# A hybrid mixer and expert layer: x is also given by channels, and the first norm's root is applied to the products' outputs

## The chip, the core and the metric

The kernel runs on one core of a Trainium2 chip. The metric is the device time of one execution in microseconds (us); what is compared are medians of several executions. The core's engines each work through a queue of their own in program order: TensorE (PE; its weight loads, PEld, overlap its products), VectorE (DVE), ScalarE (ACT), GpSimd (POOL) and SyncE (SP, which here only issues DMAs). They wait for each other by semaphores. Products land in PSUM, everything else lives in SBUF.

## What is computed

One layer over 1024 tokens of 1024 channels, in float32:

```python
hn = rmsnorm(x, norm_mix)                       # x * rsqrt(mean(x*x) + eps) * g
proj = hn @ w_in                                # 6160 columns: z, xbc, dt, sc_b, sc_c, sc_v
xbc = silu(causal_conv4(xbc) + b)               # 1536 channels: xs, B, C of the scan
dt  = softplus(dt_raw + dt_bias)                # 16 heads
y   = ssd_scan(xs, dt, -exp(a_log), B, C) + d_skip * xs
ssd = grouped_rmsnorm(y * silu(z), 2 groups)
sc  = grouped_rmsnorm(sc_b * causal_conv3(sc_c * sc_v), 16 groups)
h   = x + concat(ssd, sc) @ w_out
hn2 = rmsnorm(h, norm_ffn)                      # router: best of 4 groups, best 2 of its 8 experts
out = rmsnorm(h + sum_of_two(gate * expert(hn2)), final_norm)
```

The root of the first norm is one number per token. A product's output is linear in it, so it can be applied before the product, to x, or after it, to the outputs; `norm_mix` is one number per channel and goes onto x either way.

## The kernel before, in words

**Halves and blocks.** The tokens are worked in two halves of 512 (`TB`). A half of the mixer is 61 blocks, built by `add_blocks` (lines 123 to 143): one for `dt`, 12 for `xbc`, 24 for `c`, `v`, `b` (two each in turn), 8 for `z`, and 16 for `w_out` (`s` and `d`, four and four). A block is 24 products of 128x128 by 128x512 (the `dt` block has 16 narrow ones). Each matrix element is split into a high and a low half (`split_w`, lines 159 to 169: ACT copies the high half, DVE subtracts for the low half), and three products, high-high, high-low, low-high, make up one (`mm_block`, lines 255 to 260). The first half's blocks are 0 to 60, the second half's 61 to 121; blocks 62 to 73 are the second half's conv blocks, 75 the second of its `c` blocks.

**The order.** The loop at line 918 writes the order of every engine by hand. In step n it emits, in this order: `xbc_silu` of the conv output before last; the post step of block n-1 (`xbc_post` and so on, line 916); block n's products; the load of the weights to come and `split_w(n + 3)`; then the list `todo[n]`, filled by `at(n, function)` in lines 861 to 914, where `b0` is 1 for the first half and 62 for the second. PSUM has four banks for block outputs (`acc`), three for everything small (`sd`) and one (`sm`); weights have four buffers `W0` to `W3`, and `temp()` has four buffers too. So PE can run about three blocks ahead of the engines that empty its banks and split its weights, and not further.

**The conv blocks.** `xbc_post` (lines 365 to 379): ACT's `Identity` reads the block's output in PSUM with the last tap and the bias, then DVE adds the other three taps by three `scalar_tensor_tensor` (`stt`, line 84), in the second half also three short ones for the history. `dt_turn` and `dt_soft` (lines 306 to 342) make the step sizes, `cum_mm` and `cum_out` (346 to 362) their running sums. While the second half's conv blocks run, the first half's routing is done on the same engines (`h_root`, `h_rows`, `h_cols`, `route_choose`, `route_gates`, `route_pos`; `e0` is 64).

**The scan.** Per 128 tokens and group, `ssd_t` transposes, `ssd_decay` (ACT) makes the decay, `ssd_e` (DVE) the operands, `ssd_m` the products, `ssd_post` (DVE) the sums, one step each (lines 866 to 872). The first `ssd_m` of the second half stands behind block 77.

**The short conv.** `c_post` (391) copies a block to SBUF on ACT, `v_post` multiplies it in; `sc_root` (427 to 435) takes the root of the group sums, writes it to HBM and reads it back over all partitions (`rb_d` to `RB`); `sc_norm_out` waits for that.

**x.** It is read in three places. At the start four loads bring the first half by rows (`load_x`, 103); per 128 tokens ACT sums the squares, root and reciprocal follow, DVE scales the rows (`prep_stats`, `prep_root`, `prep_scale`, 226 to 234), and PE transposes them 128x128 at a time (`transpose_in`, 240, for `XT`), the eight groups of four interleaved with the `dt` products (288 to 299). For the second half the same is done at b0+46 to b0+59 of the first. And the residual: `x_load` (573) loads 128 columns of x by rows into ring 0, `x_turn` (576) transposes them on PE and copies them to ring 1 on ACT, and `o_post` (583) adds the block of `w_out` to them; `h_turn` (612) turns the sum back to rows.

**After the mixer** come 32 experts, whose weights (6 MB each) are loaded ahead by `load_m` and `reuse` (825 to 845) into every region that has come free, through the same SP queue that loads x and the weights before.

The root, as it stands in the kernel before:

```python
def inv_root(o, i, n):
    act.activation(o, i, AF.Sqrt, bias=eps[:o.shape[0]], scale=1.0 / n)
    dve.reciprocal(o, o)
def halves(o, k, pt, scale):
    copy_a(o[:, 0, k], pt, scale=scale)
    stt(o[:, 1, k], pt, scale, o[:, 0, k].bitcast(F32), OP.mult, OP.subtract)
```

Of the kernel before, what the change touches and what calls it, by code (L numbers as in the profile page):

```python
# [11 lines left out]
AF = mybir.ActivationFunctionType  # L12
OP = mybir.AluOpType
# [22 lines left out]
@with_exitstack  # L36
def layer(ctx: ExitStack, tc: tile.TileContext, x, norm_mix, w_in, ssd_conv_w, ssd_conv_b, dt_bias,
          a_log, d_skip, ssd_norm, sc_conv_w, sc_norm, w_out, norm_ffn, w_router_group,
          w_router_expert, w_gate, w_up, w_down, final_norm, out):
    nc = tc.nc  # L40
    x, out = x[0], out[0]
    w_in, w_out = w_in[0], w_out[0]
# [8 lines left out]
    def C(shape, name, dt=F32):  # L51
        return cst.tile(shape, dt, name=name)

    def region(tag, shape, dt=F32):
        return rg.tile(shape, dt, name=tag, tag=tag)

    def temp():
        return tk.tile([P, 512], F32, name="tk")

    def junk():  # L60
        return tk.tile([P, D], BF, name="junk", tag="tk")
# [4 lines left out]
    def sd_bank():  # L66
        return ps.tile([P, 512], F32, name="sd", bufs=3)
# [30 lines left out]
    acc_d = dr.tile([T, D], F32, name="acc_d")  # L98


    X = {}

    def load_x(h, tag):
        t = region(tag, [P, NT, D])
        for i in range(NT):
            sp.dma_start(t[:, i], x[h * TB + i * P:h * TB + (i + 1) * P, :])
        return t

    X[0] = load_x(0, "SC")
    prow = temp()  # L110
    prow = prow[:, :P]
    for o, n, src in ((0, 8, norm_mix), (8, 48, ssd_conv_w), (56, 12, ssd_conv_b), (68, 8, ssd_norm),
                      (76, 24, sc_conv_w), (100, 8, sc_norm), (108, 8, norm_ffn)):
        sp.dma_start(prow[o:o + n, :], bass.AP(tensor=src.tensor, offset=src.offset, ap=[[P, n], [1, P]]))

    WR = region("WR", [P, 2, 2048])
    W = [region(f"W{i}", [P, 2, 1024], FR) for i in range(4)]

# [26 lines left out]
    def load_w(s):  # L145
        if s < len(loads):
            src, k = loads[s]
            n = k * src.shape[1]
            sp.dma_start(WR[:, s % 2, 0:n].rearrange("p (k c) -> p k c", k=k), src.rearrange("(k p) c -> p k c", p=P))
# [19 lines left out]
            tt(o[1], raw_w(b), o[0].bitcast(F32), OP.subtract)  # L169

    load_w(0)
    load_w(1)
    dtb = C([P, H], "dtb")
    av = C([P, H], "av")
    dsk = C([P, H], "dsk")
# [41 lines left out]
    g2 = C([P, D], "g2")  # L217
    lg = C([P, NT, 36], "lg")

    pc = C([P, 116], "pc")  # L220

    def PC(i):
        return pc[:, i:i + 1]


    def prep_stats(h, i, o=None):
        act.activation(junk() if o is None else o, X[h][:, i], AF.Square, accum_out=ssx[:, h * 4 + i:h * 4 + i + 1])

    def prep_root(h, a, b):
        s = slice(h * 4 + a, h * 4 + b)  # L230
        inv_root(rsx[:, s], ssx[:, s], D)

    def prep_scale(h, i):
        dve.tensor_scalar(X[h][:, i], X[h][:, i], rsx[:, h * 4 + i:h * 4 + i + 1], None, op0=OP.mult)

    def halves(o, k, pt, scale):
        copy_a(o[:, 0, k], pt, scale=scale)
# [37 lines left out]
                pe.matmul(o[i], t[:, 1, k, c], w[:, 0, q], start=False, stop=k == KD - 1)  # L275


    pt = sd_bank()
    pe.transpose(pt[:, 0:116], prow[0:116, :], ident[0:116, 0:116])
    sq = region("Y", [P, NT, D])  # L280
    for i in range(NT):
        prep_stats(0, i, sq[:, i])
        prep_root(0, i, i + 1)
        prep_scale(0, i)
    dve.tensor_copy(pc, pt[:, 0:116])
    XT[0] = region(TA_IN[0], [P, 2, KD, TB], FR)
    DT0 = acc_bank()
    for k in range(KD):
        transpose_in(X[0], k, XT[0], PC(k))
        if k == 0:  # L290
            split_w(0)
            load_w(2)
        elif k == 4:
            split_w(1)
        if k > 1:
            mm_dt(DT0, 0, XT[0], k - 2)
    split_w(2)
    for k in (KD - 2, KD - 1):
# [20 lines left out]
    def dt_soft(h, pt):  # L319
        dts = temp()  # L320
        dt1, dt2, dt3 = (dts[:, i * 64:(i + 1) * 64] for i in range(3))
        pv = pt[:, :128].rearrange("p (c h) -> p c h", c=NT)
        tt(v64(dt1), pv[:, :, 0:H], b64(dtb), OP.add)
        tt(v64(dt1), v64(dt1), pv[:, :, H:2 * H], OP.add)
        stt(dt2, dt1, -1.0, dt1, OP.mult, OP.min)
        act.activation(dt2, dt2, AF.Exp)
        if h == 0:
            act.activation(av, av, AF.Exp)
            dve.tensor_scalar(av, av, -1.0, None, op0=OP.mult)
        dve.tensor_scalar(dt3, dt2, 1.0, None, op0=OP.add)  # L330
# [34 lines left out]
    def xbc_post(h, i, pt):  # L365
        o = XB[h][:, i]

        def w(q):
            return PC(8 + q * 12 + i)

        act.activation(o, pt, AF.Identity, bias=PC(56 + i), scale=w(3))
        for s in (1, 2, 3):
            stt(o[:, s:], pt[:, :TB - s], w(3 - s), o[:, s:], OP.mult, OP.add)
        if h == 0:
            dve.tensor_copy(hist[:, i], pt[:, TB - 3:])
        else:
# [13 lines left out]

    def c_post(h, j, pt):
        CSB[j] = temp()
        copy_a(CSB[j], pt)

    def v_post(h, j, pt):
        t = U["cv"][:, j % 2]
# [29 lines left out]

    def sc_root(h):
        gs = temp()[0:16, :]
        inv_root(gs, SUM.pop(h)[0:16, :], 64)
        pool.dma_start(rb_d[h * 16:(h + 1) * 16, :], gs)  # L430
        RB[h] = region("P1", [P, KD, TB])
        for s in range(2):
            src = rb_d[h * 16 + s:h * 16 + s + 1, :]
            pool.dma_start(RB[h][s * 64:(s + 1) * 64],
                           bass.AP(tensor=src.tensor, offset=src.offset, ap=[[0, 64], [2 * TB, KD], [1, TB]]))
# [90 lines left out]
    def z_post(h, j, pt):  # L526
        if j % 4 == 3:
            for i in range(NT):
                zs = temp()
                act.activation(zs, pt[i], AF.Silu)  # L530
                y = Y[h][:, i, j // 4 * 512:(j // 4 + 1) * 512]
                tt(y, y, zs, OP.mult)

# [37 lines left out]
        return t[h * TB:(h + 1) * TB, j * P:(j + 1) * P].rearrange("(i p) c -> p i c", p=P)  # L571

    def x_load(h, j):
        sp.dma_start(rows(ring(0, j)), dram_cols(x, h, j))

    def x_turn(h, j):
        pt = sd_bank()
        xr = ring(0, j)
        for i in range(NT):
            pe.transpose(pt[:, i * P:(i + 1) * P], xr[:, i * P:(i + 1) * P], ident)  # L580
        copy_a(ring(1, j), pt)

    def o_post(h, j, pt):
        tt(ring(1, j), ring(1, j), pt, OP.add)
# [276 lines left out]
    for h in range(2):  # L861
# [4 lines left out]
        for u in range(8):  # L866
# [15 lines left out]
        at(b0 + 43, o_room, h)  # L882
        for j in range(8):
            nd = b0 + 48 + j + (4 if j > 3 else 0)
            at(nd - 2, x_load, h, j)
            at(nd - 1, x_turn, h, j)
        if h == 1:
            for q, n in enumerate((44, 44, 45, 46, 51, 47, 49, 55, 56, 57, 57, 58, 58)):
                at(b0 + n, load_m, q)
            at(b0 + 50, h_diag)  # L890
        if h == 0:
            at(b0 + 46, lambda: X.__setitem__(1, load_x(1, "SC")))
            for i in range(NT):
                at(b0 + 50 + i // 2, prep_stats, 1, i)
            at(b0 + 52, prep_root, 1, 0, 4)
            for i in range(NT):
                at(b0 + 53, prep_scale, 1, i)
            at(b0 + 56, lambda: XT.__setitem__(1, region(TA_IN[1], [P, 2, KD, TB], FR)))
            for k in range(KD):
                at(b0 + 56 + k // 2, lambda k=k: transpose_in(X[1], k, XT[1], PC(k)))  # L900
            at(b0 + 28, route_load)
            at(b0 + 37, route_const)
            at(b0 + 46, route_weights)
            e0 = b0 + HB + 2
            at(e0 + 1, h_root, 0)
# [409 lines left out]
```

## Time and profile before

| | |
|---|---|
| median of 3 executions | 1434.77 us (1433.69 to 1438.48) |
| profiled execution | 1434.36 us, of which the span 1432.5 us |
| granted TensorE clock, mean over the span | 0.985 |
| PE, DVE, ACT, POOL busy | 95%, 72%, 63%, 10% |
| HBM read, written | 309.04 MB, 29.49 MB |

A row of the timeline is start, duration, engine, line of the kernel, operation, out<-in, shapes, count; what is in brackets is the idle time of the engine just before and what ended it. Rows of like instructions that follow each other are merged. A product's duration runs to its modelled end and overlaps the next one, so the cost of a product is the distance of two starts. `tt`, `stt` and `copy_a` are helpers, so that L87, L84 and L81 stand for many places: the tile names tell them apart. A tile is named by its region: P stands for the regions P1 and P2 (`seg`, `xw`, the rings), SC, Y, TA, TB for theirs, `tk` for a temp.

### The profile page before, as it was taken

How to read it: one execution, taken by the hardware profiler on the slowest of the kernel's cores; microseconds unless marked ns; L12 is line 12 of the kernel's file. 1: busy time of each engine (PE TensorE's matmuls, PEld its weight loads, DVE VectorE, ACT ScalarE, POOL GpSimd, SP SyncE). 2: the span in 40 equal slices, each digit the busy share in tenths (PEclk: the TensorE clock that was granted, in tenths of full speed). 3: DMA queues.
4: the chain of work that ended last, by engine and by line, in shares of the span. 5: the costliest groups of instructions: out<-in, count | busy, mean ns of one | idle time of the engine just before them, and what ended most of it. 6: DMA issues, size and time to landing. Idle time of an engine off the chain costs nothing. (4 is left out here: it accounts for less than half of the span.)

```text
span 1432.5 us, 17523 instructions
## 1 busy us (share of the span) xinstructions
PE 1364.8 (95%) x6467; PEld 1080.3 (75%) x6467; DVE 1036.5 (72%) x1357; ACT 895.4 (63%) x1344; POOL 139.0 (10%) x128
## 2 busy tenths in 40 slices
PE   6999999999999999999999699999999999999992
PEld 4888888878878878888788576777777777777771
DVE  5755676664367776755643588999999999999884
ACT  5655434355465644343643577788888888888884
POOL 0000010200000000000000101211111111111110
PEclk9999999999999999999999899999999999999996
DMA  6323332453444232324655779899999999997996
GB/s 193 134 91 115 102 108 89 117 179 106 138 153 134 89 118 89 103 89 126 227 188 168 277 294 339 317 361 361 356 372 364 351 360 378 387 375 275 367 369 249
DMA packets 130533, 322.67 MB, mean 225 GB/s; under 512 B 11039, under 2 KB 91091, under 8 KB 105868
## 3 DMA queue, kind: packets, MB, share of 16 engines
q1 hardware_dynamic: 117164, 291.06, 55.7%
q0 software_dynamic: 13280, 30.45, 8.4%
q8 instruction: 52, 0.85, 0.2%
q14 instruction: 37, 0.30, 0.1%
HBM read 309.04 MB, written 29.49 MB: 236 GB/s over the span
## 5 line engine op out<-in xcount | busy, mean ns | idle before, releaser
L87 DVE TENSOR_TENSOR W<-WR,W 128x1024 fp32r<-128x1024 f32 (+1 forms) x162 | 195.2, 1210 | 108.5 <-ACT W L81 108.2
L1150 PE MATMUL acc<-W,TB 128*112 128x512 f32 x512 | 205.3, 401 | 0.0
L1151 PE MATMUL acc<-W,TB 128*112 128x512 f32 x512 | 201.6, 394 | 2.7 <-DVE W L87 2.7
L1152 PE MATMUL acc<-W,TB 128*112 128x512 f32 x512 | 203.3, 397 | 0.0
L81 ACT ACTIVATE W<-WR 128x1024 fp32r<-128x1024 f32 (+1 forms) x162 | 168.4, 1043 | 34.1 <-PE acc L275 18.3
L258 PE MATMUL acc<-TA,W 128*128 128x512 f32 x416 | 165.5, 398 | 2.0 <-ACT tk L530 2.0
L258 PE MATMUL acc<-TB,W 128*128 128x512 f32 x416 | 166.0, 399 | 1.4 <-ACT tk L530 1.4
L260 PE MATMUL acc<-TA,W 128*128 128x512 f32 x416 | 162.3, 390 | 0.0
L260 PE MATMUL acc<-TB,W 128*128 128x512 f32 x416 | 162.3, 390 | 0.0
L259 PE MATMUL acc<-TA,W 128*128 128x512 f32 x416 | 162.1, 390 | 0.0
L259 PE MATMUL acc<-TB,W 128*128 128x512 f32 x416 | 162.0, 389 | 0.0
L87 DVE TENSOR_TENSOR W<-SC,W 128x1024 fp32r<-128x1024 f32 x96 | 114.3, 1219 | 16.7 <-ACT W L81 16.4
L87 DVE TENSOR_TENSOR W<-Y,W 128x1024 fp32r<-128x1024 f32 x92 | 109.4, 1218 | 11.5 <-ACT W L81 11.4
L1151 PEld LDWEIGHTS acc<-W,TB 128*112 128x112 f32 x512 | 90.3, 176 | 32.0 <-DVE W L87 3.6
L1152 PEld LDWEIGHTS acc<-W,TB 128*112 128x112 f32 x512 | 89.6, 175 | 29.5 <-DVE TB L87 0.2
L1150 PEld LDWEIGHTS acc<-W,TB 128*112 128x112 f32 x512 | 89.8, 175 | 27.5 <-ACT TB L81 0.2
L1162 PE MATMUL sd<-W,TB 128*112 128x512 f32 x256 | 101.3, 396 | 3.2 <-DVE W L87 3.2
L81 ACT ACTIVATE W<-SC 128x1024 fp32r<-128x1024 f32 x96 | 98.4, 1058 | 9.4 <-PE sd L1163 2.4
L87 DVE TENSOR_TENSOR W<-P,W 128x1024 fp32r<-128x1024 f32 x80 | 95.3, 1218 | 12.5 <-ACT W L81 12.5
L1161 PE MATMUL sd<-W,TB 128*112 128x512 f32 x256 | 103.5, 404 | 0.6 <-ACT TB L81 0.6
L1163 PE MATMUL sd<-W,TB 128*112 128x512 f32 x256 | 101.7, 397 | 0.0
L81 ACT ACTIVATE W<-Y 128x1024 fp32r<-128x1024 f32 x92 | 94.8, 1059 | 10.8 <-PE sd L1163 3.9
(316 smaller groups left out, 2486.3 us busy)
## 6 DMA issues: line engine op xcount, KB each, us to landing
WR<-in_w_in_dram SPq DMA_DIRECT2D x44, 1024.0 KB, 5.0
SC<-in_w_down_dram SPq DMA_DIRECT2D x18, 1024.0 KB, 7.4
WR<-in_w_out_dram SPq DMA_DIRECT2D x16, 1024.0 KB, 6.6
SC<-in_w_gate_dram SPq DMA_DIRECT2D x16, 1024.0 KB, 7.6
P<-in_w_up_dram SPq DMA_DIRECT2D x16, 1024.0 KB, 7.6
Y<-in_w_up_dram SPq DMA_DIRECT2D x16, 1024.0 KB, 8.0
Y<-in_w_gate_dram SPq DMA_DIRECT2D x15, 1024.0 KB, 8.3
TA<-in_w_down_dram SPq DMA_DIRECT2D x15, 1024.0 KB, 6.8
```

Source lines behind the costliest of these rows:

```text
L81: act.activation(o, i, AF.Copy, scale=scale)
L87: dve.tensor_tensor(o, a, b, op=op)
L258: pe.matmul(o, w[:, 0, k], t[:, 0, k], start=start and k == 0, stop=False)
L259: pe.matmul(o, w[:, 0, k], t[:, 1, k], start=False, stop=False)
L260: pe.matmul(o, w[:, 1, k], t[:, 0, k], start=False, stop=stop and k == KD - 1)
L1150: pe.matmul(pt, a[:, 0, k], w[:, 0, q], start=k == 0, stop=False)
L1151: pe.matmul(pt, a[:, 0, k], w[:, 1, q], start=False, stop=False)
L1152: pe.matmul(pt, a[:, 1, k], w[:, 0, q], start=False, stop=k == KD - 1)
L1161: pe.matmul(pt, a[:, 0, k], w[:, 0, n], start=k == 0, stop=False)
L1162: pe.matmul(pt, a[:, 0, k], w[:, 1, n], start=False, stop=False)
L1163: pe.matmul(pt, a[:, 1, k], w[:, 0, n], start=False, stop=k == 3)
```

## The change

x is passed to the kernel a second time as its transpose (`xT`, 1024 channels by 1024 tokens), and the small vectors as one 128x116 table (`small`). Both are laid out before the launch. The tokens' high and low halves (`XT`) are made straight from the loaded channels with `norm_mix`, without the norm's root. The rows of x are still loaded, for the sums of squares only: the first half's into region Y behind the first weights, the second half's into P2 at the start too. `root_rows` spreads the root over all partitions (a diagonal of it times a matrix of ones) and keeps it and its square in `ROOT`, which lies in the buffer of `g2`; `g2` is loaded later, once per half (`g2_load`, split off `route_load`). The root is then applied to the outputs of the blocks: `xbc`, `dt` and `z` by the root, `c` by its square (for `c` times `v`), and the group sums of the short conv by both (for `b`). The residual is loaded by channels into ring 1.

```diff
--- before.py
+++ after.py
+    pc = C([P, 116], "pc")
+    sp.dma_start(pc, small)
...
+    def load_xT(h, k, n):
+        sp.dma_start(X[h][:, k:k + n], xT[k * P:(k + n) * P, h * TB:(h + 1) * TB].rearrange("(k p) t -> p k t", p=P))
+
+    def load_rows(h, tag):
+        t = ROWS[h] = region(tag, [P, NT, D])
         for i in range(NT):
             sp.dma_start(t[:, i], x[h * TB + i * P:h * TB + (i + 1) * P, :])
...
+    X[0] = region("SC", [P, KD, TB])
...
     load_w(0)
+    for k in range(KD):
+        load_xT(0, k, 1)
     load_w(1)
+    load_rows(0, "Y")
...
-    def prep_scale(h, i):
-        dve.tensor_scalar(X[h][:, i], X[h][:, i], rsx[:, h * 4 + i:h * 4 + i + 1], None, op0=OP.mult)
+    ROOT = g2.rearrange("p (s t) -> p s t", s=2)
+
+    def root_rows(h):
+        pt = sd_bank()
+        for i in range(NT):
+            d = temp()[:, 0:P]
+            dve.tensor_scalar(d, ident, rsx[:, h * 4 + i:h * 4 + i + 1], None, op0=OP.mult)
+            pe.matmul(pt[:, i * P:(i + 1) * P], ones, d, start=True, stop=True)
+        copy_a(ROOT[:, 0], pt)
+        act.activation(ROOT[:, 1], pt, AF.Square)
...
-    for i in range(NT):
-        prep_stats(0, i, sq[:, i])
-        prep_root(0, i, i + 1)
-        prep_scale(0, i)
...
-        transpose_in(X[0], k, XT[0], PC(k))
+        halves(XT[0], k, X[0][:, k], PC(k))
...
+    for i in range(NT):
+        prep_stats(0, i)
+    prep_root(0, 0, 4)
+    root_rows(0)
+    load_rows(1, "P2")
...
-        tt(v64(dt1), pv[:, :, 0:H], b64(dtb), OP.add)
-        tt(v64(dt1), v64(dt1), pv[:, :, H:2 * H], OP.add)
+        r = rsx[:, h * 4:h * 4 + 4][:, :, None].to_broadcast([P, NT, H])
+        tt(v64(dt1), pv[:, :, 0:H], r, OP.mult)
+        tt(v64(dt2), pv[:, :, H:2 * H], r, OP.mult)
+        tt(v64(dt1), v64(dt1), b64(dtb), OP.add)
+        tt(dt1, dt1, dt2, OP.add)
...
+        t = temp()
+        tt(t, pt, ROOT[:, 0], OP.mult)
+        pt = t
         act.activation(o, pt, AF.Identity, bias=PC(56 + i), scale=w(3))
...
-        copy_a(CSB[j], pt)
+        tt(CSB[j], pt, ROOT[:, 1], OP.mult)
...
-        inv_root(gs, SUM.pop(h)[0:16, :], 64)
+        tt(gs, SUM.pop(h)[0:16, :], ROOT[0:16, 1], OP.mult)
+        inv_root(gs, gs, 64)
+        tt(gs, gs, ROOT[0:16, 0], OP.mult)
...
-                act.activation(zs, pt[i], AF.Silu)
+                act.activation(zs, pt[i], AF.Silu, scale=rsx[:, h * 4 + i:h * 4 + i + 1])
...
-        sp.dma_start(rows(ring(0, j)), dram_cols(x, h, j))
-    def x_turn(h, j):
-        pt = sd_bank()
-        xr = ring(0, j)
-        for i in range(NT):
-            pe.transpose(pt[:, i * P:(i + 1) * P], xr[:, i * P:(i + 1) * P], ident)
-        copy_a(ring(1, j), pt)
+        sp.dma_start(ring(1, j), xT[j * P:(j + 1) * P, h * TB:(h + 1) * TB])
...
+        at(b0 + 40, g2_load)
+        if h:
+            at(b0, root_rows, 1)
...
-            at(nd - 2, x_load, h, j)
-            at(nd - 1, x_turn, h, j)
+            at(nd - 1, x_load, h, j)
...
-            at(b0 + 46, lambda: X.__setitem__(1, load_x(1, "SC")))
+            at(b0 + 46, lambda: X.__setitem__(1, region("SC", [P, KD, TB])))
+            at(b0 + 46, load_xT, 1, 0, 4)
+            at(b0 + 46, load_xT, 1, 4, 4)
...
-                at(b0 + 50 + i // 2, prep_stats, 1, i)
-            at(b0 + 52, prep_root, 1, 0, 4)
-            for i in range(NT):
-                at(b0 + 53, prep_scale, 1, i)
+                at(b0 + 2 + i, prep_stats, 1, i)
+            at(b0 + 6, prep_root, 1, 0, 4)
...
-                at(b0 + 56 + k // 2, lambda k=k: transpose_in(X[1], k, XT[1], PC(k)))
+                at(b0 + 56 + k // 2, lambda k=k: halves(XT[1], k, X[1][:, k], PC(k)))
```

## Rows read from the trace of the kernel before

**Rows 1.** page, part 1: busy us (share of the span) xinstructions of each engine

```profile
PE 1364.8 (95%) x6467; PEld 1080.3 (75%) x6467; DVE 1036.5 (72%) x1357; ACT 895.4 (63%) x1344; POOL 139.0 (10%) x128
```

**Rows 2.** waits of PE, 0 to 790 us: who waited for whom: total, times, longest

```profile
PE acc L258 <- ACT tk L530: 3.4, 2, 2.0
...
PE sd L580 <- DVE TA L84: 0.7, 1, 0.7
...
PE sd L466 <- DVE Y L87: 0.5, 1, 0.5
```

**Rows 3.** windows: stretch, length, busy us (xinstructions), PEclk, DMA share, GB/s

```profile
60.00:98.00 38.00, 38.00 (x170) 31.45 (x169) 23.77 (x35) 16.59 (x22) 0.00 (x0) 1.00 0.37 124
450.00:495.00 45.00, 45.00 (x224) 37.55 (x223) 41.40 (x101) 21.09 (x29) 1.65 (x3) 1.00 0.33 110
```

**Rows 4.** timeline of PE at the first half's last `d` blocks

```profile
379.08 0.60 PE L580 MATMUL sd<-ident,P 128*128 128x128 f32 x4
379.44 0.48 PE L258 MATMUL acc<-TA,W 128*128 128x512 f32 x1
...
385.44 1.04 PE L243 MATMUL sd<-ident,SC 128*128 128x128 f32 x8
386.23 0.48 PE L258 MATMUL acc<-TA,W 128*128 128x512 f32 x1
```

**Rows 5.** timeline of PE: the first product of block 1

```profile
24.25 0.39 PE L258 MATMUL acc<-TA,W 128*128 128x512 f32 x1
```

**Rows 6.** windows of the start

```profile
2.00:6.00 4.00, 0.00 (x0) 0.00 (x0) 0.09 (x1) 1.80 (x6) 1.69 (x3) 1.00 0.93 350
6.00:11.50 5.50, 0.00 (x0) 0.00 (x0) 2.65 (x6) 2.65 (x6) 0.00 (x0) 1.00 0.81 138
11.50:13.00 1.50, 0.00 (x0) 0.00 (x0) 0.02 (x1) 1.44 (x3) 0.00 (x0) 1.00 0.14 30
```

**Rows 7.** timeline of ACT at the start: the last sum of squares

```profile
11.53 1.06 ACT L227 ACTIVATE Y<-SC 128x1024 f32<-128x1024 f32 x1 [0.99 <-DMA SC<-in_x_dram]
```

**Rows 8.** timeline of PE: block 75 begins; first `ssd_m` of the second half

```profile
487.34 0.49 PE L258 MATMUL acc<-TB,W 128*128 128x512 f32 x1
...
506.17 1.89 PE L497 MATMUL sd<-P,P 128*128 128x64 f32 x16
```

**Rows 9.** windows at the change from mixer to experts

```profile
806.40:816.90 10.50, 2.34 (x21) 2.04 (x20) 5.63 (x26) 5.13 (x17) 1.11 (x1) 0.50 0.68 251
816.90:820.00 3.10, 3.06 (x12) 2.44 (x13) 1.34 (x4) 1.09 (x2) 0.00 (x0) 0.50 0.02 5
```

**Rows 10.** timeline of DVE, second half, conv blocks to first `v` block

```profile
449.80 2.32 DVE L84 SCALAR_TENSOR_TENSOR TA<-acc,pc,TA 128x511 f32<-128x511 f32 x3 [2.39 <-ACT TA L371]
...
481.55 2.31 DVE L84 SCALAR_TENSOR_TENSOR TA<-acc,pc,TA 128x511 f32<-128x511 f32 x3
...
485.92 2.32 DVE L84 SCALAR_TENSOR_TENSOR TA<-acc,pc,TA 128x511 f32<-128x511 f32 x3 [0.29 <-ACT TA L371]
...
504.20 0.69 DVE L87 TENSOR_TENSOR P<-sd,dtt 128x512 f32<-128x512 f32 x1
...
506.06 0.68 DVE L87 TENSOR_TENSOR P<-acc,tk 128x512 f32<-128x512 f32 x1
...
507.54 0.75 DVE L84 SCALAR_TENSOR_TENSOR SC<-P,pc,SC 128x512 f32<-128x512 f32 x1 [0.79 <-ACT SC L81]
```

**Rows 11.** lines by form, 413.5 to 520 us: group xcount | busy, mean ns | idle

```profile
L84 DVE SCALAR_TENSOR_TENSOR TA<-acc,pc,TA 128x511 f32<-128x511 f32 x12 | 9.0, 747 | 8.6 <-ACT TA L371 8.6
...
L84 DVE SCALAR_TENSOR_TENSOR SC<-P,pc,SC 128x512 f32<-128x512 f32 x4 | 3.0, 752 | 2.5 <-ACT SC L81 2.4
...
L626 ACT ACTIVATE junk<-P 128x128 bf16<-128x128 f32 x6 | 1.8, 308 | 0.2
...
L81 ACT ACTIVATE tk<-acc 128x512 f32<-128x512 f32 x2 | 1.2, 578 | 0.0
```

**Rows 12.** waits of the whole run: DVE for the broadcast root

```profile
DVE SC L84 <- DMA P<-rb_d: 5.4, 2, 3.4
```

More of the change, by code (lines that the diff above doesn't have):

```diff
@@ L38, in layer @@
           a_log, d_skip, ssd_norm, sc_conv_w, sc_norm, w_out, norm_ffn, w_router_group,
-          w_router_expert, w_gate, w_up, w_down, final_norm, out):
+          w_router_expert, w_gate, w_up, w_down, final_norm, xT, small, out):
     nc = tc.nc
@@ L98, in layer, with PC @@
     acc_d = dr.tile([T, D], F32, name="acc_d")
+    pc = C([P, 116], "pc")
+    sp.dma_start(pc, small)
+    def PC(i):
+        return pc[:, i:i + 1]
     X = {}
-    def load_x(h, tag):
-        t = region(tag, [P, NT, D])
+    def load_xT(h, k, n):
+        sp.dma_start(X[h][:, k:k + n], xT[k * P:(k + n) * P, h * TB:(h + 1) * TB].rearrange("(k p) t -> p k t", p=P))
+    ROWS = {}
+    def load_rows(h, tag):
+        t = ROWS[h] = region(tag, [P, NT, D])
         for i in range(NT):
             sp.dma_start(t[:, i], x[h * TB + i * P:h * TB + (i + 1) * P, :])
[L107 to L114, printed above, removed]
+    X[0] = region("SC", [P, KD, TB])
     WR = region("WR", [P, 2, 2048])
@@ L218, in layer, with prep_stats @@
     lg = C([P, NT, 36], "lg")
[L220 to L227, printed above, removed]
+    def prep_stats(h, i):
+        act.activation(junk(), ROWS[h][:, i], AF.Square, accum_out=ssx[:, h * 4 + i:h * 4 + i + 1])
     def prep_root(h, a, b):
@@ L275, in mm_z @@
                 pe.matmul(o[i], t[:, 1, k, c], w[:, 0, q], start=False, stop=k == KD - 1)
-    pt = sd_bank()
-    pe.transpose(pt[:, 0:116], prow[0:116, :], ident[0:116, 0:116])
-    sq = region("Y", [P, NT, D])
-    for i in range(NT):
-        prep_stats(0, i, sq[:, i])
-        prep_root(0, i, i + 1)
-        prep_scale(0, i)
-    dve.tensor_copy(pc, pt[:, 0:116])
     XT[0] = region(TA_IN[0], [P, 2, KD, TB], FR)
@@ L573, in x_load @@
     def x_load(h, j):
-        sp.dma_start(rows(ring(0, j)), dram_cols(x, h, j))
-    def x_turn(h, j):
-        pt = sd_bank()
-        xr = ring(0, j)
-        for i in range(NT):
-            pe.transpose(pt[:, i * P:(i + 1) * P], xr[:, i * P:(i + 1) * P], ident)
-        copy_a(ring(1, j), pt)
+        sp.dma_start(ring(1, j), xT[j * P:(j + 1) * P, h * TB:(h + 1) * TB])
     def o_post(h, j, pt):
@@ L661, in route_load, with g2_load @@
             pool.dma_start(wr[:, :, o:o + n], src.rearrange("(k p) e -> p k e", p=P))
+    def g2_load():
         pool.dma_start(g2, row_bcast(norm_ffn, D))
@@ L1307 @@
         args.append(nc.dram_tensor(f"in_{name}_dram", a.shape, mybir.dt.from_np(a.dtype), kind="ExternalInput").ap())
+    small = [inputs[n][0].reshape(-1, P) for n in ("norm_mix", "ssd_conv_w", "ssd_conv_b", "ssd_norm", "sc_conv_w",
+                                                   "sc_norm", "norm_ffn")]
+    for name, a in (("xT", inputs["x"][0].T), ("small", np.concatenate(small).T)):
+        a = np.ascontiguousarray(a)
+        arrays[f"in_{name}_dram"] = a
+        args.append(nc.dram_tensor(f"in_{name}_dram", a.shape, mybir.dt.from_np(a.dtype), kind="ExternalInput").ap())
     for i, (shape, dtype) in enumerate(_OUTS):
```

## The prediction

> **What bounds the kernel now.** The page's first part comes first: PE is busy 95% of the span, the other engines 72% or less [rows 1]. The view of waits, PE's over the mixer (0 to 790 us), shows how real that is: behind the start there is almost nothing in it, two waits on the gate's Silu, 3.4 us together, and 0.7 us before x_turn's first transposes in each half (the row from TA; its twin from TB is the same) [rows 2]. So from 24 us to about 800 us the order of PE is the time: a PE instruction that goes is saved, a PE wait that comes is paid. The experts after that keep their program and their order; I shift them as a block.
>
> The windows show who is next. In the first half's conv blocks DVE works 23.77 of 38 us; in the second half's, between 450 and 495 us, 41.40 of 45 [rows 3], because the router's choice for the first half, softplus and the cumulative sums stand in its queue there. That stage decides this change.
>
> **What goes from PE.** x_turn: 16 groups of four transposes, each taking 0.36 us from its start to the next block's [rows 4]: 5.8 us, and with it the two waits of 0.7 us before the first of them, 1.4 us [rows 2]. The eight groups that turn x for the second half: 0.79 us per two, 3.2 us [rows 4]. Together **-10.4 us** (between -9 and -11: the waits may stay). The ACT copies behind x_turn go too and were hidden. x_load now writes ring 1 directly, one block later than x_load did; it waits for h_turn three columns back, done long before, has a block of 5.4 us to land (170 products in 38 us, so 24 in 5.4 [rows 3]), and SP no longer stands at x_turn's end with the expert loads behind it. Zero, both for this and for 2 KB pieces instead of 512 B.
>
> **The start.** Before, PE begins block 1 at 24.25 us [rows 5]; the norm's four steps ran as x arrived. After, root_rows puts four products with `ones` into PE's queue ahead of block 1, and these need the sums of squares of all rows, which are loaded last: small constants, W 0.5 MB, x 2 MB, W 1 MB, rows 2 MB on one queue, 5.6 MB. Before, the 4.6 MB up to W's second megabyte arrived by about 21.3 us, with a hole at 11.5 to 13 (30 GB/s: W was issued late) and a slow stretch at 6 to 11.5 (138 GB/s, while POOL's three broadcasts run) [rows 6]. The broadcasts stay, the hole goes: 4.6 MB by 19.8, the last megabyte at 350 GB/s [rows 6] by 22.8. Then the last Square, 1.06 [rows 7], and about 1 for its sum, root, reciprocal and the first scaled identity: 24.9. Four fp32 products, two passes each: 16 passes of 64 columns take 1.89 us to their end [rows 8], so for eight of 128 I estimate 0.9; between 0.4 and 1.8. PE has then idled since the dt products. [...] Block 1 is where it would have been at 27.35: **+3.1 us**. Bounds: -4 if all 5.6 MB come at 350 GB/s from 2 us on, +5 if the slow stretch lasts.
>
> [...]
>
> **The conv blocks.** xbc_post was ACT's Identity from PSUM, then three multiply-adds on DVE. Now a DVE product with ROOT stands ahead of Identity, so DVE must hand over to ACT and wait for it. Such a hop is in the trace: v_post's product starts at 506.06, ACT scales, the next DVE instruction starts at 507.54: 1.48 us [rows 10]. Behind it stand the multiply-adds, the next split's low half (which PE needs three blocks later) and the router's steps.
>
> First half: DVE had 38 - 23.77 = 14.2 us free in seven blocks [rows 3], 2.0 us each, against 1.48: the lag of dt_soft is worked off more slowly, nothing reaches PE. prep_stats there, four times about 1.25 us, and two more table loads lie on ACT, busy 16.59 of 38 [rows 3]: zero; without that cover about 2 us.
>
> Second half: with DVE late, a post came every 4.37 us (481.55 to 485.92), 0.29 of it idle [rows 10], so 4.1 us of work; after, 4.1 + 1.48 = 5.6, no longer under PE's 5.4: DVE can't catch up what softplus, sums and router put in. Post by post. The first waits for ROOT: root_rows' products after block 62 (1.0 us on PE, where its fourth scaled identity reuses a buffer), then on ACT the copy and the Square of ROOT, 0.58 each, and four of h_stats' Squares of 0.31 with their sums [rows 11], then the hop: about +3.8. Two posts (one at 449.80, its twin just before it) pay nothing: DVE stood 2.39 us for ACT's tables already [rows 10], and the product fits in. Where DVE waited 0.29 a post pays 1.2; where router steps stood ahead, Identity was ready and it pays the whole 1.5. Up to the tenth post: 3.8 + 3 x 1.2 + 4 x 1.5 = 13.4; the last two, 1.2 each: 15.8.
>
> Who waits for it. Block 75's low half stands between those two posts and was done where the 0.29 begins, at 485.63 [rows 10]; PE reached the block at 487.34 [rows 8] and needs it with the third product, 0.45 later. Now 499.0, so the block starts at 498.6: **+11.2** (1.0 of it root_rows; block 74 pays part of it). Then the first ssd products: their operand was ready at 504.20 + 0.69 [rows 10], 1.3 before PE came at 506.17 [rows 8]. Now 15.8 later, less two ACT copies of 0.58 that c_post takes off ACT's queue ahead of it: 519.5, against 506.17 + 11.2: **+2.1**. ssd_post is late by the same 1.2 beyond PE, and the transposes behind it already waited 0.5 [rows 2]: **+1.2**. Sum **+14.5 us**. Bounds: +2, if only the product's 0.68 in eight saturated blocks counts and the 3.6 us that DVE had free between 450 and 495 [rows 3] take most of it; +17, if nothing is absorbed. I take 14.5, since the hop and the due times are measured rows.
>
> [...]
>
> **c_post, sc_root, the rest.** c_post's 16 products move from ACT (0.58) to DVE (0.68) [rows 10, 11]; after the catch-up PE waits for neither in that stage [rows 2], zero (up to 2). sc_root gets two products around its chain and no longer begins until ssd_post's DVE work is through: 0.7 + hop + 0.7, the chain ends about 2.2 us later. It feeds the broadcast that sc_norm_out waited for already, 3.4 us in one half and 2.0 in the other [rows 12]; behind that stand y_stats and the Silu that PE waits for, 3.4 [rows 2]. In the second half all 2.2 arrive; in the first about 1.5, since ACT also stood for a W load. **+3.7 us**; 0 to 6, the upper end if g2's reload, 0.5 MB behind the broadcast, holds up W too. dt_soft's added multiply (0.2) is in the lag. z's scale operand, split halves from SBUF: zero.
>
> **Sum.** -10.4 + 3.1 + 14.5 + 3.7 = +10.9. The profiled execution took 1434.36 (span 1432.5 and 1.9 around it), 0.4 below the median of 1434.77. Predicted: **1445.3 us**. About 0.3%, 4.3 us, is what a measurement here can tell from no change.
>
> **Rivals.**
> (a) DVE's lag is absorbed: its queue, between 450 and 495 us, decides. For it: one free block before block 75 and ACT only half busy; against it: 1.7 and 1.3 us of slack. With the lower bound of +2 the sum is -1.6: 1432.8, no change. Chance 0.18.
> (b) The removed transposes are the whole story: (a) and the start at its lower bound as well, since the loads are issued without the hole: 1434.4 - 10.4 - 4 + 2 + 3.7 = 1425.7, faster. Against it: rows last in the queue. It is decided by whether the rows land before 17 us. Chance 0.12.
> (c) The transfers collide: the broadcast, g2 and W in front of z, and the start at its upper bound: 1445.3 + 2.3 + 1.9 + 2.5 of the bound above the 14.5: 1452. For it: the start's 138 GB/s [rows 6]. Chance 0.15.
> (d) It doesn't do what it says: x_load, one block later, lands behind two expert loads of 1 MB and o_post waits, about 3 us (1 MB at 350 GB/s [rows 6]) in the second half: 1448. Against it: SP is then freed earlier. Chance 0.05.
> The forecast itself: 0.50, with 1439 to 1449 as its own range.
>
> **How the numbers follow.** Slower by over 0.3% (above 1439): forecast, (c), (d): 0.70. Within: (a), 0.18. Faster: (b), 0.12. The range must reach into (a) and (c): 1432 to 1453.
>
> **What would show it.** Right: PE's view of waits in the second half names DVE's split and the ssd operands near 490 to 520 us, over 10 us in all; DVE has a wait on ACT's Identity of some 0.8 us before each conv post; no PE wait in the first half's conv blocks; block 1 begins at 26 to 27 us behind root_rows; L580 and its two waits are gone. Wrong: PE runs through 450 to 520 us as before, or block 1 begins below 21 us.

## The result, and the profile after

The changed kernel takes 1459.1 us (median of 4 executions, 1457.64 to 1460.87) against 1436.6 us (1433.69 to 1438.54) for the kernel before, with one execution more than in the section on the time before: ratio 1.0159, 95% interval [1.0134, 1.0183]. Forecast were 1445.3 us and a range up to 1453. The direction was right, the size was not. The profiled spans are 1457.8 and 1432.5 us, so 25.3 us are to be explained; by the medians it is 22.5, because the profiled executions lie 2.3 us below their median (before) and 0.5 above (after).

Page of the changed kernel, part 1; beside [rows 1] PE is busy 9 us longer, while it has 113 instructions fewer:

```profile
PE 1373.6 (94%) x6354; PEld 1073.5 (74%) x6354; DVE 1060.4 (73%) x1401; ACT 887.3 (61%) x1315; POOL 139.7 (10%) x129
```

PE's waits, 0 to 790 us (total, times, longest), to be read beside [rows 2]:

```profile
PE acc L269 <- ACT tk L546: 7.7, 2, 5.5
...
PE sd L774 <- DVE M L87: 4.1, 1, 4.1
PE sd L483 <- DVE tab L813: 3.9, 1, 3.9
PE sd L243 <- DVE tk L242: 3.6, 1, 3.6
PE acc L271 <- DVE W L87: 1.5, 1, 1.5
```

The Silu wait of [rows 2] grew from 3.4 to 7.7 us. L774 (the router's counts), L483 (the scan's transposes, behind the router's table) and L271 (a low half of the weights) are new; all three end on DVE, between 470 and 516 us; L243 is root_rows at the start. x_turn's two waits are gone.

Windows (columns as in [rows 3]): the two stretches of rows 3 again (the changed kernel is some 6 us later in its program in the second), and one behind the 5.5 us wait:

```profile
60.00:98.00 38.00, 38.00 (x169) 31.47 (x168) 28.64 (x47) 23.82 (x33) 2.31 (x5) 1.00 0.41 136
313.50:317.50 4.00, 4.00 (x11) 3.13 (x10) 3.57 (x6) 3.94 (x9) 0.00 (x0) 0.50 0.00 0
...
450.00:495.00 45.00, 40.89 (x176) 32.51 (x175) 35.13 (x86) 21.43 (x29) 2.20 (x4) 0.92 0.33 107
```

In the first half PE stays full (38.00 of 38). In the second half's conv blocks PE has 176 instructions where it had 224, and DVE is *less* busy than before (35.13 against 41.40): it waits. And the granted clock, 1.00 in both windows before, is 0.50 from 313.50 to 317.50 us, behind the 5.5 us wait.

Where it was lost: starts of the same PE instruction in the two timelines.

| PE instruction | before | after | later by | step |
|---|---|---|---|---|
| first half: `dt_turn` | 35.24 | 40.54 | 5.30 | start +5.3 |
| first `s` block | 303.52 | 312.90 | 9.38 | wait for z's Silu +4.1 |
| first transposes of `y_out` | 314.54 | 326.60 | 12.06 | behind that wait +2.7 |
| second half: `dt_turn` | 424.60 | 430.73 | 6.13 | x_turn and transposes -8.0, root_rows +1.0, products +1.1 |
| second `ssd_t` | 516.58 | 538.19 | 21.61 | conv stage +15.5 |
| `ssd_m`, seventh of the half | 633.88 | 657.80 | 23.93 | products +2.3, no wait |
| first `s` block | 697.59 | 723.21 | 25.62 | products +1.4, wait for Silu +0.3 |
| first transposes of `y_out` | 708.61 | 735.86 | 27.25 | behind that wait +1.6 |
| first expert's transposes | 816.94 | 839.70 | 22.76 | x_turn -4.5 |
| end of the span | 1432.5 | 1457.8 | 25.3 | experts +2.5 |

Where a step has several parts, they are sums of the distances from one start to the next, by kind of instruction. The second half's wait for z's Silu itself grew only from 2.03 to 2.28 us. So six of these steps hold a growth that the waits above don't explain: the two "behind that wait", the three marked "products" (1.1, 2.3 and 1.4 us), and the experts' 2.5.

### The profile page after: what moved, and what is told of

It reads as the page before. It is cut to its first block, busy times and chain, and to the rows that moved or that the text cites. A ratio compares the mean times of both kernels' runs of the same rounds, so it can differ in the third digit from the quotient of the medians.

```text
span 1457.8 us, 17306 instructions
## 1 busy us (share of the span) xinstructions
PE 1373.6 (94%) x6354; PEld 1073.5 (74%) x6354; DVE 1060.4 (73%) x1401; ACT 887.3 (61%) x1315; POOL 139.7 (10%) x129
## 5 line engine op out<-in xcount | busy, mean ns | idle before, releaser
L269 PE MATMUL acc<-TB,W 128*128 128x512 f32 x416 | 170.6, 410 | 5.5 <-ACT tk L546 5.5
L271 PE MATMUL acc<-TB,W 128*128 128x512 f32 x416 | 166.9, 401 | 1.5 <-DVE W L87 1.5
L270 PE MATMUL acc<-TB,W 128*128 128x512 f32 x416 | 166.9, 401 | 0.0
L271 PE MATMUL acc<-TA,W 128*128 128x512 f32 x416 | 163.6, 393 | 0.0
```

Source lines behind the costliest of these rows:

```text
L269: pe.matmul(o, w[:, 0, k], t[:, 0, k], start=start and k == 0, stop=False)
L270: pe.matmul(o, w[:, 0, k], t[:, 1, k], start=False, stop=False)
L271: pe.matmul(o, w[:, 1, k], t[:, 0, k], start=False, stop=stop and k == KD - 1)
```

## The experiments

**The conv post: hop or work?** Three kernels with other products in `xbc_post`, and one without:

```diff
# e2_no_product
-        t = temp()
-        tt(t, pt, ROOT[:, 0], OP.mult)
-        pt = t
# e1_unused_product
-        pt = t
# e1b_work_without_hop
-        tt(t, pt, ROOT[:, 0], OP.mult)
-        pt = t
+        tt(t, ROOT[:, 1], ROOT[:, 0], OP.mult)
# e1c_hop_without_work
-        tt(t, pt, ROOT[:, 0], OP.mult)
-        pt = t
+        tt(t[:, 0:1], pt[:, 0:1], ROOT[:, 0, 0:1], OP.mult)
```

e2: 

> The changed kernel without the product in xbc_post (the root is left out of xbc). Both theories: the second half's conv stage loses only root_rows' 1.0 us and at most 1 us more against before; about 1444 us. What this one adds to e1_unused_product is the price of the product's work alone: 0 to 3 us by 'the hop', 8 us or more by 'the work'. If the stage stays 10 us behind, its cause is neither, but root_rows' gate or the router.

e1: 

> The changed kernel, but xbc_post's DVE product goes to a tile that nothing reads: Identity and the multiply-adds read PSUM, as before the change (the root is left out of xbc). DVE keeps the product's 0.68 us, the hand-over to ACT and back (0.89 us of idle DVE in each post of the changed kernel) goes. Theory 'the hop': of the some 15.5 us that PE falls behind between 424 and 538 us, 10 or more come back; about 1447 us, and DVE shows no wait of 0.89 us on ACT's Identity. Rival 'the work': DVE was full in that stage, so 0.68 us a post is enough to keep it behind: 1455 us or more, and PE still stalls for the router's product.

e1b: 

> The changed kernel with xbc_post's product made from two SBUF rows (128x512 from ROOT and ROOT) into a tile that nothing reads; Identity and the multiply-adds read PSUM, so ACT no longer waits for the product (the root is left out of xbc). e1_unused_product had kept that wait, because two engines' readings of one PSUM tile are put in order: 0.85 us of idle DVE in each post stayed, and 13.7 of the 16.6 us between the changed kernel and e2_no_product with it. Theory 'the hop': without the wait most of that goes: 1444 to 1448 us. Rival 'the work': the product's 0.68 us of DVE are what PE waits for: 1453 us or more.

e1c: 

> The changed kernel with xbc_post's product cut to one column (128x1) into a tile that nothing reads; Identity still waits for it, and the multiply-adds for Identity (the root is left out of xbc). Theory 'the hop': DVE idles 0.85 us a post as before, and the time stays within 5 us of e1_unused_product: 1451 to 1456 us. Rival 'the work': near e2_no_product, 1443 to 1446 us. If both this and e1b_work_without_hop lie halfway, the two add up.

| kernel | us | ratio to before | above e2 | PE's waits, 420 to 540 us |
|---|---|---|---|---|
| e2, neither | 1442.5 | 1.0042 [1.0025, 1.0059] | | 0 |
| e1b, work alone | 1446.5 | 1.0078 [1.0054, 1.0102] | 4.0 | 3.0 |
| e1c, hop alone | 1451.5 | 1.0109 [1.0087, 1.0132] | 9.0 | 5.5 |
| e1, both | 1456.1 | 1.0136 [1.0119, 1.0152] | 13.7 | 9.0 |
| the changed kernel | 1459.1 | 1.0159 [1.0134, 1.0183] | 16.6 | 9.5 |

e1 missed its aim: its Identity still waited for the DVE product, though it read only PSUM. In e1 both read one PSUM tile, and Identity starts behind the product (436.74 us, the product runs from 436.02 to 436.70); in e1b, whose product reads SBUF, it doesn't wait for it. e1 has 13.3 us of idle DVE ahead of 12 posts' first multiply-adds, e1b 5.2. DVE's lines by form, 424 to 525 us, of e1c, then of e1b and of e2 (group xcount | busy, mean ns | idle before them):

```profile
L84 DVE SCALAR_TENSOR_TENSOR TA<-acc,pc,TA 128x511 f32<-128x511 f32 x12 | 9.0, 750 | 15.1 <-ACT TA L384 15.1
```

```profile
L84 DVE SCALAR_TENSOR_TENSOR TA<-acc,pc,TA 128x511 f32<-128x511 f32 x12 | 9.0, 746 | 5.2 <-ACT TA L384 5.2
...
L87 DVE TENSOR_TENSOR tk<-g 128x512 f32<-128x512 f32 x12 | 8.2, 684 | 1.7 <-ACT g L245 1.7
```

```profile
L84 DVE SCALAR_TENSOR_TENSOR TA<-acc,pc,TA 128x511 f32<-128x511 f32 x12 | 9.0, 747 | 10.0 <-ACT TA L382 10.0
```

Over 12 posts, e1c idles 15.1 us for Identity; e2 10.0, which it can afford, since it has no product; e1b turns half of that idle time into its 8.2 us of products. So the work alone half fits into idle time and costs 4.0, the hop alone (with the 0.15 us of its one-column product in each post) costs 9.0, and they add up: neither theory has all of it. The intervals of e1b and e2 just overlap; that the work costs something, PE's waits show. From e1 to the changed kernel 3.0 us are left; why isn't shown, and the profiled e1 was 1.6 ahead already at the first half's `dt_turn`.

**The start.** In e3 root_rows(0) goes behind block 1:

```diff
# e3_root_behind_block1
-    root_rows(0)
...
-        if h:
-            at(b0, root_rows, 1)
+        at(b0, root_rows, h)
```

> The changed kernel with root_rows(0) emitted behind block 1's products instead of ahead of them (nothing left out). Theory 'the rows gate the start': block 1 begins right behind the dt products (last one at 21.65 us in the changed kernel), by 23 us instead of 27.6, root_rows' 1 us comes later: 3 to 5 us less, 1455 us. Rival 'the loads of x and W gate the start': block 1 can't begin before 26 us, 1459 us, no change.

1454.9 us, 1.0133 [1.0116, 1.0149]: 4.2 less. Block 1 begins at 22.04 us and `dt_turn` at 36.21. So the gate was root_rows. PE of the changed kernel there:

```profile
25.91 2.05 PE L243 MATMUL sd<-tk,ones 128*128 128x128 f32 x8 [3.63 <-DVE tk L242]
27.61 0.77 PE L269 MATMUL acc<-TA,W 128*128 128x512 f32 x1
28.18 0.63 PE L270 MATMUL acc<-TA,W 128*128 128x512 f32 x1
28.61 0.63 PE L271 MATMUL acc<-TA,W 128*128 128x512 f32 x1
```

The four products took 1.7 us, and the first products of block 1 stand 0.43 us apart.

**What a wait costs behind itself.** e5 puts useless products where PE waits for z's Silu:

```diff
# e5_products_in_the_stall
+    def warm(b, t, n):
+        o = sd_bank()
+        w = W[b % 4].rearrange("p s (k c) -> p s k c", k=KD)
+        for i in range(n):
+            pe.matmul(o, w[:, 0, i % KD], t[:, 0, i % KD], start=i == 0, stop=i == n - 1)
...
+        at(b0 + 43, lambda h=h, n=b0 + 43: warm(n, XT[h], 10 if h else 22))
```

> The changed kernel with 22 extra products (128x128 by 128x512, into a small PSUM bank, not used) behind the first half's last z block and 10 behind the second half's, where PE waits 5.5 and 2.3 us for z's Silu; nothing left out. Theory 'a stall costs more than its length': the extra products fill the waits, the clock is not lowered behind them (2.2 and 1.4 us of products at 0.43 us apart instead of 0.227 go), and the products behind them keep 0.227 us instead of 0.233: faster by 3 to 8 us, 1451 to 1456 us, with more work. Rival: the clock and the pitch have other causes: 1459 us or, where the products don't fit into the wait, up to 1462.

1456.1 us, 1.0138 [1.0116, 1.0160]: 3.0 less, with 32 products *more*. PE of the changed kernel behind the wait, and of e5 at the same place:

```profile
312.90 0.79 PE L269 MATMUL acc<-TB,W 128*128 128x512 f32 x1 [5.47 <-ACT tk L546]
313.49 0.63 PE L270 MATMUL acc<-TB,W 128*128 128x512 f32 x1
313.92 0.63 PE L271 MATMUL acc<-TB,W 128*128 128x512 f32 x1
```

```profile
306.71 5.15 PE L546 MATMUL sd<-TA,W 128*128 128x512 f32 x22
312.34 0.50 PE L269 MATMUL acc<-TB,W 128*128 128x512 f32 x1 [0.48 <-ACT tk L552]
312.68 0.40 PE L270 MATMUL acc<-TB,W 128*128 128x512 f32 x1
312.91 0.39 PE L271 MATMUL acc<-TB,W 128*128 128x512 f32 x1
```

The block starts when it did, but at once at 0.23 us a product instead of 0.43: counted from the last z product, `y_out` comes 2.4 us earlier, and 1.6 in the other half. So the steps "behind that wait" are the lower clock, but for some 0.3 us of the first. The granted clock was 0.50 behind the 5.47 us wait, with the products 0.43 us apart. The prediction had counted a lower clock at the start alone. Not behind every wait was it lower: behind 2.03 us for the same Silu the kernel before kept 1.00, while 0.50 came 1.2 us behind waits of 2.28 (changed kernel, second half) and 1.79 us (e12, first half). Half of e5's expectation fell: behind the wait the products still stand 0.233 us apart, not 0.227. That has another cause.

**The slower products.** e6 is the kernel before with the residual change alone; e7 adds the second half's x by channels with the root put onto x, so that no output needs it:

```diff
# e6_before_residual_channels
-        sp.dma_start(rows(ring(0, j)), dram_cols(x, h, j))
-    def x_turn(h, j):
...
+        sp.dma_start(ring(1, j), xT[j * P:(j + 1) * P, h * TB:(h + 1) * TB])
# e7_root_on_x, beside e6
+    load_rows(1, "P2")
...
+            at(b0 + 46, load_xT, 1, 0, 4)
+            at(b0 + 46, load_xT, 1, 4, 4)
...
+            at(b0 + 48, root_rows, 1)
+            for k in range(KD):
+                at(b0 + 52 + k // 2, lambda k=k: tt(X[1][:, k], X[1][:, k], R["root"], OP.mult))
```

e6: 

> The kernel before, with the residual loaded by channels and nothing else (x_turn's 64 transposes and its copies gone, x_load one block later). The prediction's price for that: 5.8 us of PE and the two waits of 0.7: 7.2 us less than before, 0.995 of it. Rival: x_load, one block later, lands late and o_post waits, 3 us given back: 0.997. If it is 1.000, PE was not the time in that stage.

e7: 

> e6_before_residual_channels, and the second half's x loaded by channels too, with the root multiplied onto it before it is split (eight DVE products of 0.68 us where DVE has room), so that no output needs it; the eight groups of transposes go, root_rows' four products come, the first half's start stays as it was before the change. Nothing left out. Against e6's 1423.2 us: 3.2 us of PE less, 1.0 more: 1421 us. Rival: the 2 MB of rows, loaded at the start, delay the first weights: 1424 us or more.

e6: 1423.2 us, 0.9917 [0.9897, 0.9937], better than expected. e7: 1429.9 us, 0.9959 [0.9945, 0.9973], *worse* than e6 with less for PE to do. It has no new wait and no fall of the clock in the mixer, yet its second-half products stand 0.2333 us apart, as in the changed kernel, and e6's 0.2267. In both slow kernels it is always the products with an operand in TB, never those on TA. In most blocks TB holds the moving operand. In the second half's z blocks it holds the stationary one, W moves, and the products are slow all the same; these are the z blocks of the kernel before, then of the changed kernel, seven products each:

```profile
659.81 0.39 PE L275 MATMUL acc<-W,TB 128*128 128x512 f32 x1
...
661.17 0.39 PE L275 MATMUL acc<-W,TB 128*128 128x512 f32 x1
```

```profile
718.66 0.40 PE L284 MATMUL acc<-W,TB 128*128 128x512 f32 x1
...
720.06 0.40 PE L284 MATMUL acc<-W,TB 128*128 128x512 f32 x1
```

Six distances are 1.36 and 1.40 us. Both slow kernels load the second half's rows into P2 at the start, ahead of the first use of TB; regions get their addresses in the order in which they are first claimed, so TB moved from byte 147360 of a partition to 163776 (the built programs' addresses). Four kernels on that alone:

```diff
# e9_TB_placed_as_before (changed kernel), e8a_root_on_x_TB_first (e7)
+    region("TB", [P, 2, KD, TB], FR)
     load_rows(1, "P2")
# e8b_root_on_x_TB_32_bytes (e7)
-            p2 = region("P2", [P, 2 * (TB + 2) + 6 * 512])
+            p2 = region("P2", [P, 2 * (TB + 2) + 6 * 512 + 8])
...
# e11_before_TB_shifted (kernel before)
+    region("PAD", [P, 8])
     def dt_post(h, j, pt):
```

e9: 

> The changed kernel with the region TB claimed ahead of P2, so that it lies at byte 147360 of a partition, as before the change, and not at 163776 (the load of the second half's rows into P2 had claimed P2 first); nothing else, nothing left out. In the changed kernel products whose moving operand lies in TB stand 0.2333 us apart (first half's s blocks, all second-half blocks on XT and SST), those on TA 0.2267, and e7_root_on_x shows the same without any stall. Theory 'the place of TB': the pitch is 0.2267 everywhere in the mixer, 4 to 6 us less there, 1 to 2 in the experts: 1452 to 1454 us. Rival 'the stall at 307 us sets the pitch': the pitch stays 0.2333 behind it: 1459 us.

e8a: 

> e7_root_on_x with TB claimed ahead of P2, at byte 147360 as in the kernel before. By the place of TB: 5 us of slow products go from e7's 1429.9 and the experts give 1.5: 1422 to 1424 us, equal to e6 or 1 to 2 below it (2.2 us of PE less in it). Rival: the extra 2 MB of rows or the root's products are what e7 loses: 1428 us or more.

e8b: 

> e7_root_on_x with P2 made 32 bytes longer, so that TB lies at byte 163808 instead of 163776: the same neighbours and order, only 32 bytes on (the weights W0 to W3, TA, and TB before the change all lie at 32 modulo 64, TB after it at 0). Theory 'alignment': the pitch is 0.2267 in TB again, 1422 to 1424 us. Rival 'region of the memory': 0.2333 stays, 1429 us.

e11: 

> The kernel before with 32 unused bytes in front of TB, so that TB, P1 and P2 lie 32 bytes on (TB at byte 147392 of a partition instead of 147360), and not one instruction changed. Theory 'the place of TB sets the pitch of its products': products on TB go from 0.2267 us to 0.2333, 5 to 7 us slower, 1441 to 1443 us. Rival 'it is not the address but the change of neighbours or of order': 1436 us, pitch 0.2267.

PE of the changed kernel, of e9 and of e11, inside a block of the second half:

```profile
553.93 0.40 PE L270 MATMUL acc<-TB,W 128*128 128x512 f32 x1
554.17 0.40 PE L271 MATMUL acc<-TB,W 128*128 128x512 f32 x1
554.40 0.39 PE L269 MATMUL acc<-TB,W 128*128 128x512 f32 x1
554.63 0.40 PE L270 MATMUL acc<-TB,W 128*128 128x512 f32 x1
```

```profile
551.24 0.39 PE L269 MATMUL acc<-TB,W 128*128 128x512 f32 x1
551.47 0.39 PE L270 MATMUL acc<-TB,W 128*128 128x512 f32 x1
551.70 0.39 PE L271 MATMUL acc<-TB,W 128*128 128x512 f32 x1
551.92 0.39 PE L269 MATMUL acc<-TB,W 128*128 128x512 f32 x1
```

```profile
550.89 0.40 PE L259 MATMUL acc<-TB,W 128*128 128x512 f32 x1
551.13 0.39 PE L260 MATMUL acc<-TB,W 128*128 128x512 f32 x1
551.36 0.40 PE L258 MATMUL acc<-TB,W 128*128 128x512 f32 x1
551.60 0.39 PE L259 MATMUL acc<-TB,W 128*128 128x512 f32 x1
```

Three products take 0.70, 0.68 and 0.71 us. The durations (0.39 or 0.40) hide it, the starts show it. Over the 650 to 730 distances under 0.3 us on TB between 430 and 640 us, the mean is 0.2333 in the changed kernel and in e11, 0.2273 in the kernel before and 0.2275 in e9; on TA, between 100 and 250 us, it is 0.2274 to 0.2276 in all four.

| kernel | TB at byte | us apart, TB moving | TB stationary (z) | us | ratio to before |
|---|---|---|---|---|---|
| e9, changed kernel | 147360 | 0.2267 | 0.2269 | 1452.3 | 1.0113 [1.0095, 1.0131] |
| e8a, e7 | 147360 | 0.2267 | 0.2270 | 1422.0 | 0.9898 [0.9878, 0.9918] |
| e8b, e7 | 163808 | 0.229 to 0.231 | 0.2332 | 1424.0 | 0.9917 [0.9898, 0.9936] |
| e11, kernel before | 147392 | 0.2333 | 0.2333 | 1441.8 | 1.0036 [1.0022, 1.0050] |

e11 has the instructions of the kernel before, one by one, and is 5.4 us slower. e9 takes 6.8 off the changed kernel. So the place is shown as the cause; the rule is not: both slow places are multiples of 64 bytes and the fast one 32 more, but e8b, 32 more as well, lies between with TB moving and is as slow as any with TB stationary.

**The chain to z.** e4b has sc_root as before and g2_load at b0+46; e4c only changes the queue and step of g2's load:

```diff
# e4c_g2_on_sync
-        pool.dma_start(g2, row_bcast(norm_ffn, D))
+        sp.dma_start(g2, row_bcast(norm_ffn, D))
...
-        at(b0 + 40, g2_load)
+        at(b0 + 46, g2_load)
```

e4b: 

> The changed kernel with sc_root as before (the root is left out of the short conv's group sums) and g2 loaded six blocks later, behind z. Theory of the prediction's step (two products and a hop in the chain to z's Silu, and g2 in front of a weight load): PE's wait of 5.5 us at 307 us falls back to 1.5 and that of 2.3 at 723 us to 1 to 2; with them go the products at half the clock behind the waits, 2.2 and 1.4 us: 8 us in all, 1450 to 1452 us. Rival: the broadcast collides with the weight loads in any case and the waits stay above 3 us: 1456 us or more.

e4c: 

> The changed kernel with g2's 0.5 MB loaded from SyncE's queue six blocks later, behind the first half's weights for the s blocks, in place of GpSimd's queue; sc_root keeps its two products; nothing left out. Theory 'g2 in front of the weights': the 1.3 us by which ScalarE waited longer for the weight load go, PE's wait of 5.5 us at 307 us becomes 4.2, the clock still falls behind it: 1 to 2 us less, 1457 to 1458 us. Rival 'the broadcast itself fills the DMA engines': no change, 1459 us.

e4b: 1455.4 us, 1.0134 [1.0115, 1.0153]; e4c: 1457.0, 1.0138 [1.0120, 1.0156], by its time alone not told from the changed kernel. ScalarE's split of the weights for the `s` blocks, in the changed kernel and in e4c, and PE's Silu wait in e4b and e4c:

```profile
297.23 1.06 ACT L81 ACTIVATE W<-WR 128x1024 fp32r<-128x1024 f32 x1 [1.95 <-DMA WR<-in_w_out_dram]
```

```profile
295.81 1.06 ACT L81 ACTIVATE W<-WR 128x1024 fp32r<-128x1024 f32 x1 [0.49 <-DMA WR<-in_w_out_dram]
```

```profile
PE acc L269 <- ACT tk L544: 5.0, 2, 3.6
```

```profile
PE acc L269 <- ACT tk L546: 5.8, 2, 3.9
```

Two shares of the first half's wait, 5.5 us: sc_root's products 1.9 (5.5 to 3.6), g2's transfer in front of the weights 1.5 (5.47 to 3.94). If they add, that is 3.4 of the 4.1 by which it grew; with both out, in e13 below, the wait is 2.4, 3.1 less. What the rest is, isn't shown. In the second half e4b's wait is 1.4 where the changed kernel's is 2.3, but there it varies from 1.8 (e2) to 2.7 us (e1b) in kernels that leave this chain as it is. e4b moved g2 in vain: GpSimd had nothing to wait for and still issued it at 286.0 us, ahead of the weights; its expectation missed for that reason.

**All at once.** e13 is the changed kernel with e2's, e3's and e4c's edits, sc_root as before, and TB and P1 claimed ahead of P2.

> The changed kernel without the product in xbc_post, with sc_root as before (the root is left out of xbc and of the group sums), g2 loaded from SyncE's queue behind the weights, root_rows(0) behind block 1, TB and P1 claimed ahead of P2. If the causes named are all: 1459.1 less 16.6 (the product), 6.8 (TB), 4.2 (start) and 7 to 9 (the chain to z, with the clock behind its waits) is 1422 to 1425 us, which is also 1436 less the 12.6 of the residual and 3.2 of the transposes, with 2 for root_rows. If something unnamed is left: 1428 us or more.

1425.3 us, 0.9923 [0.9906, 0.9939]: 33.8 us below the changed kernel, 0.3 above the expected stretch. Taken out one by one they gave 16.6 (e2), 6.8 (e9), 4.2 (e3), 3.7 (e4b) and 2.1 (e4c), 33.4 us together. So the causes named are the loss, within a few us.

**The best version.** e12 is e8a with P1 claimed ahead of P2 too.

> e8a_root_on_x_TB_first with P1 claimed ahead of P2 as well, so that every region lies as in the kernel before; nothing left out. As e8a, 1422 us, or up to 1 us less, if the scan's products on P1 had been slowed too; faster than the kernel before by 13 to 15 us.

1423.7 us, 0.9908 [0.9891, 0.9924], no better than e8a. e6, e8a and e12 can't be told apart; all are faster than both kernels, and e6 is the smallest edit.

## Why the prediction was wrong

It forecast +10.9 us; the profile shows +25.3 (22.5 by the medians). What failed is the price of a wait: away from the start it was taken to be the wait's length, and the products at the lower clock behind it were left out, most of all in the chain to z; and one effect, the place of TB, had no term at all. By its steps:

- **What goes from PE, -10.4: right**, a little more. In the table -8.0 and -4.5. In e6 a group of x_turn was worth 0.45 us instead of 0.36, and the first of each half 1.35 with its wait: 9.0 us instead of 7.2. (Its second Silu wait also fell, from 2.0 to 0.7 us, with no edit there; why isn't shown.)
- **The start, +3.1: undersized, +5.3.** The gate (e3) was right. The 27.35 us hold 1.8 for root_rows' products, twice the estimated 0.9, and 0.65 lost in block 1, by a clock of 0.50 over 3.1 us: so it was granted from 816.90 to 820.00 us [rows 9], after PE had stood idle from 803.00 to 806.40. No run had shown it for the start; the changed kernel's granted clock is 0.50 from 22.80 to 31.00 us, and root_rows' products took 1.7. Root_rows' products began at 25.9 instead of 24.9, since ACT took the four Squares one after the other only behind the split of x; and block 1 lost 2 us at the lower clock, not 0.65. Of the 5.3 a part may be scatter: the kernels that share this start reach `dt_turn` between 38.9 (e1) and 40.7 us (e4c).
- **First half's conv blocks, 0: right** [rows 3]: PE 38.00 of 38.
- **Second half's conv stage, +14.5: mechanism right** (e1c, e1b), **the size by luck**, 16.5 with root_rows. The new waits, 4.1, 1.5 and 3.9, are 9.5 us, where 13.5 were forecast beside root_rows; products at half the clock behind two of them add 3.8 by their starts (12 products from 476.8 and 7 from 516.5 us, each 0.2 late; granted were 0.50 from 476.50 to 481.50 and from 516.50 to 519.50 us), which had no term; the rest is root_rows, 1.0, and about 2 us of slower products on TB, which had none either. The place was partly wrong: the router's counts caught PE first, not block 75's split. In a post DVE makes the product and then idles 0.89 us for Identity, where 0.8 was forecast:

```profile
443.88 0.68 DVE L87 TENSOR_TENSOR tk<-acc,g 128x512 f32<-128x512 f32 x1
445.44 2.33 DVE L84 SCALAR_TENSOR_TENSOR TA<-tk,pc,TA 128x511 f32<-128x511 f32 x3 [0.89 <-ACT TA L385]
```

  From SBUF these multiply-adds take no less than from PSUM, 751 ns in the mean against 747 before [rows 11], so the prediction was right to leave their time as it was:

```profile
L84 DVE SCALAR_TENSOR_TENSOR TA<-tk,pc,TA 128x511 f32<-128x511 f32 x12 | 9.0, 751 | 13.8 <-ACT TA L385 13.8
```

- **The chain to z, +3.7: the step that failed.** It measures 8.6: waits longer by 4.1 and 0.3, and 2.7 and 1.6 behind them, where e5 shows the lower clock. The waits' sum, 4.3, is near the forecast, but in the wrong halves: 1.5 was forecast for the first and 2.2 for the second. The prediction named g2's load, as the upper end of 6; it took a wait's price to be its length.
- **No term: the place of TB.** `load_rows(1, "P2")` was counted as a transfer. It also claims P2 first. 6.8 us in all (e9); in the table 1.1, 2.3 and 1.4 ("products"), and the part of the conv stage above.
- **The experts, taken as unchanged, +2.5: open.** With TB stationary there, the mean distances are up by 0.3 ns over 1536 products and 1.4 ns over 768, some 1.5 us. But the stage takes anything from 614.7 to 619.3 us in these kernels, 614.7 in e1b with TB moved and 617.8 in e12 with TB as before, so that the 2.5 can't be put down to TB.

Against the forecast: start 2.2, conv 2.0, chain to z 4.9, place of TB elsewhere 4.8, experts 2.5, transposes -2.1: 14.4 with the digits left out here, which is 25.3 - 10.9. Rival (c), transfers that collide, had the right place for 1.5 us of it.

## What to carry to other kernels

Where one engine sets the time, look at the granted clock behind every wait that a change makes longer, and not just at the start: where it fell, here to 0.50 behind new waits of 2.3 to 5.5 us, the products behind cost 1.4 to 2.4 us on top of the wait's length; behind 1.5 us in the conv stage it did not fall. When a diff claims a buffer earlier than before, list the addresses of all buffers behind it. And split a change before believing its sum: here one part of it, e6, holds the whole gain, and the root on the outputs costs more than the transposes that it saves, while the second half's root on the input (e8a) can't be told from free.

## What was not expected of the hardware

Products of 128x128 by 128x512 with one operand, moving or stationary, 32 bytes further on in SBUF stand 0.2333 us apart instead of 0.2267 (e11): 2.9%. Why, and by which rule (e8b), stays open.
